# Hybrid mLSTM/HGRN2 step on one core: token halves in a new order, aligned slots, uneven value columns, and four raw weight buffers instead of five

## The chip, the cores and the metric

The kernel runs on one core of one Trainium2 chip. The time is device microseconds (us) of one execution. "Before" was timed three times: 1118.25 us in the median, 1116.19 to 1118.37. A profile is of one further execution, which has its own time. The engines are called as in the profile: PE multiplies matrices (PEld is its weight load), DVE and ACT do elementwise work, POOL does small copies and scans, and SP does nothing here but issue transfers from and to memory, one after the other: an issue that has to wait holds up those behind it.

## What is computed

One layer of a streaming encoder for 544 tokens, 32 of a running stream ("sample") and 512 of a new one ("prompt"). Cut to what matters:

```python
proj = xn @ w_in                       # 1024 -> 12296 columns: u, v, z, gates, q,f,i,g of HGRN2, ga, gb
c  = silu(causal_conv(u))
qm, km = c_head @ w_qm, c_head @ w_km * M_HD ** -0.5      # 4 heads of 512
s  = (q @ k.T) * dmat                                     # mLSTM, per head
h  = (w_inter * (C @ q) + s @ v) / max(|den|, exp(-m))
C_new = decay * C + (w_last * v).T @ k
ya = mlstm_out @ w_brm
a  = sum_c q * exp(g_t - g_s) * k                         # HGRN2, 8 heads of 128
S_new = exp(g_last) * S + (k * exp(g_last - g)).T @ v
yb = hgrn_out @ w_brh
y  = sigmoid(ga) * ya + sigmoid(gb) * yb
h  = x + y @ w_out
out = rmsnorm(h + sigmoid(h @ w_pg) * (p @ w_ple))
```

## The kernel before

**Products.** Every large product is made of three matmuls in fp32r: with each operand split in a rounded part (h) and a rest (l) it adds wh·xh, wh·xl and wl·xh in PSUM. Tokens stand on the free axis in two halves of TH = 272, so one 128 by 128 weight block is used by 272-column matmuls, three for each half.

**Weights.** A weight comes from memory in raw pieces of 128 x 512 (256 KB), `raw_piece`, L166, one SP transfer each, into a pool of NRAW = 5 buffers. The rounded part is a CAST on ACT (L183, or L196 outside the staged pump), the rest a subtraction on DVE (L188, L197). A raw buffer is free again when its last reader is through, and the next piece in the order of loading takes it; its transfer is issued on SP at that moment and not before. Where a piece lies in its ring buffer of 576 columns is set by an offset `at`; `lag` works it out from the token half's start, modulo 64 columns.

**The input projection.** `Two` multiplies two output blocks at once in seven products instead of eight, so it adds raw pieces to each other (sums s1 to s4, DVE, L531): the pieces of a pair are called a11, s2, a12, s3, s1, a22, s4, and its four raw pieces are read by those sums and by the splits. In trace names `wi52r` and `wi60r` are the raw pieces of units 52 and 60 (two each; r0 and r1 in the order rows below), `wa1152h` the rounded part of form a11 of unit 52, `ws` a sum. The matmuls are those of L573: 24 of one half, then the next form. `Onto` is a `Two` that adds to earlier results. `Pump` loads AHEAD and RAWAHEAD = 3 pieces before they are used.

**mLSTM.** For each of four heads: `stage_k` and `stage_q` (k and q, `dense`, L221), scores (L1036), `memory` (L1093, the new C of the prompt), numerators (L1272) and `sample` (L1248), then `ya` (`dense`). The value tiles have 516 columns, 512 values and a column of ones, padded, multiplied as two groups of VH = 258. `dense` goes over the 128-row blocks k, over the three products, and innermost over the two token halves. In head 0 the four raw pieces of wq (wq00, wq01) are loaded between those of the input projection.

**HGRN2.** Eight heads of about 31.4 us each, at 648 to 869 us, between which the input projection's pieces are prepared. Here the order of every instruction on ACT, DVE and PE is written out by hand. Elsewhere only PE's order is written out, or parts of it, and a scheduler orders the others. The pairs for the gates ga and gb follow (870 to 946 us, by hand as well), then the yb product, w_out, w_ple and w_pg.

**Storage.** NSLOT = 26 general slots of 550 columns hold activations (k, q, values and so on); SCRATCH sets aside 128 columns.

## Time and profile before

| | |
|---|---|
| Timed, median of 3 | 1118.25 us (1116.19 to 1118.37) |
| Profiled execution, its time / its span | 1115.95 us / 1114.2 us |
| Granted TensorE clock in it | 1.0 throughout |
| DVE, ACT, POOL busy | 919.7, 714.6, 169.5 us |
| Read and written in memory | 109.32 MB and 24.91 MB |

The span goes from the first to the last instruction; 1.75 us of the time lie around it. "Busy" of PE counts overlapping matmuls, each from its fetch to its modelled end, so it says that PE has work and not how fast it goes through it; how fast is read from the distance between starts, a piece of the chain of waits divided by its count of matmuls.

## The change

- `dense` now calls `by_half`: of a weight piece the first token half has all its matmuls, then the second. `steps`, `One.run`, `memory` and the numerators do likewise.
- Slots have 576 columns (a multiple of 64) and the weights that multiply k, q, ya and w_ple's input get the offset `in_slots` in their pieces. `Onto` gets offsets of its own for four of its forms.
- The 516 value columns are multiplied as 256 and 260 instead of 258 and 258; in two places value tiles start 16 columns further in. The copies from PSUM follow: 512 columns and the ones column taken from PSUM, and in `sample` four copies on ACT instead of two (8 more in all).
- To make room: NRAW 5 to 4, SCRATCH 128 to 32, and `wi` takes two buffers in turn instead of four tiles.
